# Block inverses in a gated DeltaNet layer: transposes that write row by row, and 32-column products on two row groups in turn

## The chip, the cores and the metric

The kernel runs on one core of a Trainium2 chip. The metric is the device time of one execution in microseconds; the median of several runs counts. One further execution was profiled, and every time inside the kernel below is from its trace.

## The reference, cut to what matters

The kernel computes a two-layer trunk for 256 tokens of width 2048: differential attention and a gated MLP with a short convolution, then a gated DeltaNet and a second such MLP. The change lies in the DeltaNet. For each of its 32 heads and each chunk of the sequence, the delta rule solves a unit lower triangular system:

```python
decay = jnp.exp(jnp.where(tril, g_c[..., :, None] - g_c[..., None, :], -jnp.inf))
low = jnp.where(strict, jnp.einsum('bhncd,bhnkd->bhnck', k_beta, k) * decay, 0.0)
a_mat = low + jnp.eye(CHUNK, dtype=low.dtype)
u = lax.linalg.triangular_solve(a_mat, v_beta, left_side=True, lower=True, unit_diagonal=True)
w = lax.linalg.triangular_solve(a_mat, k_beta * jnp.exp(g_c)[..., None], left_side=True, lower=True, unit_diagonal=True)
```

The kernel uses chunks of 128 tokens, which gives the same result, and forms the inverse of each 128 x 128 matrix instead of solving. There are 32 heads x 2 chunks = 64 such matrices.

## The kernel before, in words

**Large matmuls.** Nearly all of the work is dense: `dense` (lines 101 to 121) and `dense_tok` (127 to 142) multiply activations by weights that stream from memory in tiles of 512 KB. `weights` (line 76) issues the DMA into `raw`, ScalarE rounds it to `whi` (L88), VectorE subtracts to get `wlo` (L89), and TensorE takes three matmuls for each piece: high by high (L115), low by high (L116), high by low (L117); L137 to L139 are the same in `dense_tok`. `raw`, `whi` and `wlo` have three buffers each.

**Small work in between.** After each weight tile `dense` calls `tick` (line 71), which lets every generator in a background queue take one step. Attention, norms and the DeltaNet's own steps are such generators. So the small matmuls stand among the large ones in TensorE's program, and a `yield` is the place where large matmuls go between two dependent small steps. The program is then ordered by a scheduler with a model of the time, so that an engine's final order can differ a little from the order of the code.

**The inverses.** The DeltaNet goes through four blocks of four query heads, each query head with two value heads. Per block there are 8 value heads x 2 chunks = 16 matrices. `keys` puts the 32 x 32 diagonal pieces of all 16 matrices into one tile `Cc` of 128 partitions x 32 x 32: a partition's quarter (`quad[s]`, 32 partitions) tells which of a matrix's four diagonal pieces it holds. `invert` (line 511) transposes it on VectorE (L516), runs a substitution over 30 columns (L524, L527) and writes the result with two transposes:

- `ttc` (L531), indexed [partition, i, m]: the transposed inverses, with the matrix m last.
- `tcc` (L533), indexed [partition, c, m]: the inverses, read through a rearranged view, again with m last.

A VectorE transpose here turns every 32 x 32 piece (32 partitions by 32 elements) by itself. Since m is the last index, one matrix's row in `ttc` or `tcc` is 32 elements that lie 32 elements (128 bytes) apart.

**The levels.** `levels` (line 536) builds the full inverses from the diagonal pieces, for a group of two query heads (8 matrices) at a time, so twice per block and eight times in all:

1. GpSimd copies the diagonal pieces of the group into `TT` (L546, four quarters) and `Ta` (L548, two quarters).
2. `pp` (L552): for quarters s = 0 and s = 2, and the 8 matrices, a 32 x 32 product of a piece of `lt` with a piece of `tcc`. The result for quarter s goes to the PSUM partitions of quarter s + 1. It is copied to `pc`: quarter 1 by VectorE (L555), quarter 3 by ScalarE (L556).
3. `px` (L561): products of `pc` with `ttc`, read from quarters 1 and 3, into quarters 0 and 2. Then `py` (L565): products of `TT` with `pc`, quarter 1 alone. They go to `Ta` (L567, VectorE) and `TT` (L569, ScalarE).
4. `pq` (L573) and `pz` (L579): the 64 x 64 products of the next level, with copies L575 and L580.

In each product the first operand is loaded as weights (PEld in the profile) and the second one, the moving tile, is streamed. `tcc` in L552 and `ttc` in L561 are moving tiles; so is `pc` in L565. A *row group* is the quarter of TensorE's rows that matches the quarter of the partitions an operand is read from; a *column group* matches the quarter that the result goes to. The f32 products appear in the trace as two records each. All results of `small` are tiles `mp` of 512 f32 per partition, one PSUM bank, from a pool of four.

Of the kernel before, what the change touches and what calls it, by code (L numbers as in the profile page):

```python
# [26 lines left out]
class Trunk:  # L27
# [38 lines left out]
    def mp(self):  # L66
        return self.mps.tile([P, 512], F32, tag="mp", name="mp")
# [343 lines left out]
    def gdn(self, w_gate, w_in, w_z, w_out, nb, hb, gate_ap, const_ap, hot_ap, conv_col, ng, done):  # L411
# [7 lines left out]
        nc, tc, mp = self.nc, self.tc, self.mp  # L419
# [4 lines left out]
        with tc.tile_pool(name="gd", bufs=1) as gd:  # L424
# [16 lines left out]
            quad = [slice(32 * s, 32 * s + 32) for s in range(4)]  # L441
            flat = "p i c -> p (i c)"
            gates = {}

            def lin(ps):
                u = gd.tile([P, 2, T], F32, tag="u", name="u", bufs=2)
                self.merge(ps, u)
                return u

            def convs(u, tiles):  # L450
                c = gd.tile([P, 2, T], F32, tag="cv", name="cv", bufs=4)
                for i in range(2):
                    self.conv(c[:, i, :], u[:, i, :], [conv_col(t, tiles[i]) for t in range(4)], None)
                nc.scalar.activation(c, c, AF.Silu)  # L454
                return c
# [55 lines left out]
            def invert(cc, lqs, inv):  # L511

                while len(lqs) < 2 * hb:
                    yield
                x = gd.tile([P, 32, 32], F32, tag="s4", name="X", bufs=3)
                nc.vector.transpose(x.rearrange(flat), cc.rearrange(flat))  # L516
                t = gd.tile([P, 32, 32], F32, tag="s4", name="Ti", bufs=3)
                nc.vector.tensor_scalar(t, x, -1.0, None, ALU.mult)
                nc.vector.memset(t.rearrange(flat)[:, ::33], 1.0)
                for j in range(1, 31):  # L520
                    m = 31 - j
                    tmp = gd.tile([P, T], F32, tag="tmp", name="tmp", bufs=1)
                    w = tmp[:, :m * j].rearrange("p (i c) -> p i c", c=j)
                    nc.vector.tensor_tensor(  # L524
                        w, x[:, j + 1:, j:j + 1].to_broadcast([P, m, j]),
                        t[:, j:j + 1, :j].to_broadcast([P, m, j]), ALU.mult)
                    nc.vector.tensor_tensor(t[:, j + 1:, :j], t[:, j + 1:, :j], w, ALU.subtract)  # L527
                    if j % 3 == 0:
                        yield
                ttc = gd.tile([P, 32, 32], F32, tag="s4", name="ttc", bufs=3)  # L530
                nc.vector.transpose(ttc.rearrange(flat), t.rearrange(flat))  # L531
                tcc = gd.tile([P, 32, 32], F32, tag="s4", name="tcc", bufs=3)
                nc.vector.transpose(tcc, t.rearrange("p i c -> p c i"))  # L533
                inv += [ttc, tcc]

            def levels(TT, Ta, lts, ttc, tcc, m0):

                nm = 2 * len(lts)
                ms = slice(m0, m0 + nm)
                lview = [lt[:, :T].rearrange("p (t c) -> p t c", t=2) for lt in lts]  # L540

                def small(n):
                    return mp()[:, :nm * n].rearrange("p (m c) -> p m c", m=nm)

                for s in range(4):
                    nc.gpsimd.tensor_copy(TT[quad[s], :, quad[s]], ttc[quad[s], :, ms].rearrange("p i m -> p m i"))  # L546
                for s in range(2):
                    nc.gpsimd.tensor_copy(Ta[quad[s], :, quad[s]], tcc[quad[s], :, ms].rearrange("p c m -> p m c"))  # L548
                pp = small(32)
                for s in (0, 2):  # L550
                    for m in range(nm):
                        nc.tensor.matmul(pp[quad[s + 1], m, :], lview[m // 2][quad[s], m % 2, quad[s + 1]],  # L552
                                         tcc[quad[s], :, m0 + m], start=True, stop=True)
                pc = gd.tile([P, 2 * gv, 32], F32, tag="tmp", name="pc", bufs=1)
                nc.vector.tensor_copy(pc[quad[1]], pp[quad[1]])  # L555
                nc.scalar.copy(pc[quad[3]], pp[quad[3]])  # L556
                yield
                px = small(32)
                for s in (0, 2):
                    for m in range(nm):  # L560
                        nc.tensor.matmul(px[quad[s], m, :], pc[quad[s + 1], m, :], ttc[quad[s + 1], :, m0 + m],  # L561
                                         start=True, stop=True)
                py = small(32)
                for m in range(nm):
                    nc.tensor.matmul(py[quad[1], m, :], TT[quad[1], m, quad[1]], pc[quad[1], m, :],  # L565
                                     start=True, stop=True)
                nc.vector.tensor_scalar(Ta[quad[1], :, quad[0]], py[quad[1]], -1.0, None, ALU.mult)  # L567
                for s in (0, 2):
                    nc.scalar.mul(TT[quad[s], :, quad[s + 1]], px[quad[s]], -1.0)  # L569
                yield  # L570
                pq = small(64)
                for m in range(nm):
                    nc.tensor.matmul(pq[64:, m, :], lview[m // 2][:64, m % 2, 64:], Ta[:, m, :], start=True, stop=True)  # L573
                qs = gd.tile([P, 2 * gv, 64], F32, tag="lq", name="lq", bufs=1)
                nc.vector.tensor_copy(qs[64:], pq[64:])  # L575
                yield
                pz = small(64)
                for m in range(nm):
                    nc.tensor.matmul(pz[:64, m, :], qs[64:, m, :], TT[64:, m, 64:], start=True, stop=True)  # L579
                nc.vector.tensor_scalar(TT[:64, :, 64:], pz[:64], -1.0, None, ALU.mult)  # L580
# [11 lines left out]
            def group(gi, gr, lqs, inv, vt, ready, zts, acts):  # L592
# [5 lines left out]
                yield  # L598
                sub = lqs[2 * gr[0]:2 * gr[-1] + 2]
                yield from levels(TT, Ta, [lt for lt, _ in sub], *inv, 4 * gr[0])  # L600
                while len(ready) < len(gr):
                    yield
# [66 lines left out]
            for b in range(nb):  # L669
# [6 lines left out]
                for op, i in plan + [("v", i) for i in range(1, hb)]:  # L676
                    if op == "k":
                        hq = heads[i]
                        c = convs(lin(self.dense(w_in[hq * 2], KD, self.h_acts, HP)), (hq, nq + hq))
                        self.spawn(keys(hq, c, cc, 2 * i, lqs))  # L680
                        if i == hb - 1:
                            self.spawn(invert(cc, lqs, inv))
                    elif op == "z":
                        gr = groups[i]
                        zt = zts[i] = gd.tile([P, 2, gv, P], F32, tag="vz", name="zt", bufs=4)
                        ps = self.dense_tok(w_z[heads[gr[0]] // 2], KD, self.h_acts, 27 if b < 2 else 15)
                        for t in range(2):
                            nc.scalar.activation(zt[:, t].rearrange(flat), ps[:, t, :], AF.Silu,
                                                 scale=self.rstdc[:, t:t + 1])
                    else:  # L690
                        gi = i // gh
                        gr = groups[gi]
                        if i == gr[0]:
                            vt = gd.tile([P, 2, gv, P], F32, tag="vz", name="vt", bufs=4)
                            ready = []
                            self.spawn(group(gi, gr, lqs, inv, vt, ready, zts, acts))
                        hq = heads[i]
                        c = convs(lin(self.dense(w_in[hq * 2 + 1], KD, self.h_acts, HP)),
                                  (2 * nq + 2 * hq, 2 * nq + 2 * hq + 1))
                        self.spawn(to_tokens(c, vt, 2 * (i - gr[0]), ready))  # L700
# [204 lines left out]
```

## Time and profile before

| | us |
|---|---|
| median of 3 runs | 2669.3 |
| lowest and highest of them | 2666.23, 2669.54 |
| profiled execution, its own time | 2668.26 |
| its span, first to last instruction | 2666.5 |
| TensorE busy | 2650.4 |
| VectorE busy | 1847.8 |
| ScalarE busy | 1453.1 |
| GpSimd busy | 126.9 |

TensorE's granted clock was 0.999 in the mean. How to read the rows: in a timeline a row holds the start in us from the span's start, the length in us, engine, line, operation, tiles (written <- read), shapes and how many instructions in a row were merged; idle time before it, with what ended it, stands in brackets. In a row of groups the figures behind the bar are busy us, mean ns of one, and the idle us of the engine before them. In a table of stretches a row holds the stretch, its length, and for each engine the busy us with the number of instructions that were under way in it. PEld is the weight load. In the chain that ended last, each engine's share says how much of the span it held the end. The rows of an engine's order show a running number, line, operation, tiles and the form of the result.

### The profile page before, as it was taken

How to read it: one execution, taken by the hardware profiler on the slowest of the kernel's cores; microseconds unless marked ns; L12 is line 12 of the kernel's file. 1: busy time of each engine (PE TensorE's matmuls, PEld its weight loads, DVE VectorE, ACT ScalarE, POOL GpSimd, SP SyncE). 2: the span in 40 equal slices, each digit the busy share in tenths (PEclk: the TensorE clock that was granted, in tenths of full speed). 3: DMA queues.
4: the chain of work that ended last, by engine and by line, in shares of the span. 5: the costliest groups of instructions: out<-in, count | busy, mean ns of one | idle time of the engine just before them, and what ended most of it. 6: DMA issues, size and time to landing. Idle time of an engine off the chain costs nothing.

```text
span 2666.5 us, 53673 instructions
## 1 busy us (share of the span) xinstructions
PE 2650.4 (99%) x22352; PEld 2588.3 (97%) x22352; DVE 1847.8 (69%) x2719; ACT 1453.1 (54%) x1994; POOL 126.9 (5%) x221
## 2 busy tenths in 40 slices
PE   8999999999999999999999999999999999999999
PEld 8998899999999999999989989999999999999999
DVE  7776567777777555689787787688677777776444
ACT  6555555555555444584764674574565555554333
POOL 0000000000000000031011021021000000000000
PEclk9999999999999999999999999999999999999999
DMA  6555465665666666655354454455455655656665
GB/s 205 172 176 172 160 197 193 195 194 193 195 194 195 194 194 192 190 159 182 119 175 145 149 172 154 155 166 170 143 193 196 192 195 193 195 193 199 202 202 165
DMA packets 135461, 481.62 MB, mean 181 GB/s; under 512 B 15409, under 2 KB 18481, under 8 KB 135217
## 3 DMA queue, kind: packets, MB, share of 16 engines
q1 hardware_dynamic: 134064, 475.58, 55.6%
q8 instruction: 175, 2.87, 0.4%
q10 hardware_dynamic: 1152, 2.61, 0.3%
q14 instruction: 70, 0.57, 0.1%
HBM read 476.03 MB, written 2.10 MB: 179 GB/s over the span
## 4 chain that ended last, share of the span: by engine, by line
PE 94%; ACT 2%; DVE 2%; issue 1%; DMA 0%; POOL 0%; SPq 0%; DVEq 0%; ACTq 0%
PE ps L115 26%; PE ps L116 26%; PE ps L117 26%; PE ps L138 3%; PE ps L139 3%; PE ps L137 3%; PE mp L609 2%; DVE wlo L89 1%; ACT whi L88 1%; PE mp L225 1%; PE mp L552 1%; PE mp L561 0%; DVE cv L206 0%; ACT L454 0%; PE mp L573 0%
## 5 line engine op out<-in xcount | busy, mean ns | idle before, releaser
L89 DVE TENSOR_TENSOR wlo<-raw,whi 128x1024 fp32r<-128x1024 f32 (+2 forms) x909 | 1109.0, 1221 | 642.7 <-ACT whi L88 641.1
L88 ACT CAST whi<-raw 128x1024 fp32r<-128x1024 f32 (+2 forms) x909 | 948.4, 1044 | 1007.6 <-PE ps L117 837.8
L115 PE MATMUL ps<-h,whi 128*128 128x256 f32 x4304 | 1192.3, 277 | 8.4 <-ACT h L151 5.5
L116 PE MATMUL ps<-h,wlo 128*128 128x256 f32 x4304 | 1192.9, 277 | 3.1 <-DVE wlo L89 3.1
L117 PE MATMUL ps<-h,whi 128*128 128x256 f32 x4304 | 1191.7, 277 | 0.0
L115 PEld LDWEIGHTS ps<-h,whi 128*128 128x128 f32 x4304 | 808.8, 188 | 10.3 <-ACT h L151 5.5
L116 PEld LDWEIGHTS ps<-h,wlo 128*128 128x128 f32 x4304 | 809.4, 188 | 5.9 <-DVE wlo L89 4.0
L117 PEld LDWEIGHTS ps<-h,whi 128*128 128x128 f32 x4304 | 809.4, 188 | 0.5
L115 PE MATMUL ps<-ac,whi 128*128 128x256 f32 x1632 | 450.4, 276 | 0.0
L116 PE MATMUL ps<-ac,wlo 128*128 128x256 f32 x1632 | 450.3, 276 | 0.0
L117 PE MATMUL ps<-ac,whi 128*128 128x256 f32 x1632 | 450.2, 276 | 0.0
L115 PEld LDWEIGHTS ps<-ac,whi 128*128 128x128 f32 x1632 | 306.3, 188 | 0.0
L116 PEld LDWEIGHTS ps<-ac,wlo 128*128 128x128 f32 x1632 | 306.3, 188 | 0.0
L117 PEld LDWEIGHTS ps<-ac,whi 128*128 128x128 f32 x1632 | 306.2, 188 | 0.0
L138 PE MATMUL ps<-wlo,h 128*128 128x512 f32 x384 | 149.7, 390 | 0.2
L137 PE MATMUL ps<-whi,h 128*128 128x512 f32 x384 | 149.9, 391 | 0.0
L139 PE MATMUL ps<-whi,h 128*128 128x512 f32 x384 | 149.2, 389 | 0.0
L115 PE MATMUL ps<-oc,whi 128*128 128x256 f32 x512 | 143.9, 281 | 0.0
L117 PE MATMUL ps<-oc,whi 128*128 128x256 f32 x512 | 143.5, 280 | 0.0
L116 PE MATMUL ps<-oc,wlo 128*128 128x256 f32 x512 | 143.3, 280 | 0.0
L206 DVE SCALAR_TENSOR_TENSOR cv<-u,fcols,cv 128x255 f32<-128x255 f32 (+1 forms) x344 | 142.9, 478 | 0.0
L123 DVE TENSOR_TENSOR u<-ps,rstd 128x512 f32<-128x512 f32 x118 | 81.4, 690 | 38.2 <-PE ps L117 37.9
(202 smaller groups left out, 2232.1 us busy)
## 6 DMA issues: line engine op xcount, KB each, us to landing
raw<-w_up SPq DMA_DIRECT2D x344, 512.0 KB, 4.4
raw<-w_down SPq DMA_DIRECT2D x160, 512.0 KB, 4.1
raw<-w_in SPq DMA_DIRECT2D x128, 512.0 KB, 4.3
raw<-w_z SPq DMA_DIRECT2D x64, 512.0 KB, 3.7
raw<-w_out SPq DMA_DIRECT2D x64, 512.0 KB, 3.6
raw<-w_qk SPq DMA_DIRECT2D x63, 512.0 KB, 4.1
raw<-w_v SPq DMA_DIRECT2D x32, 512.0 KB, 3.7
raw<-w_o SPq DMA_DIRECT2D x32, 512.0 KB, 4.4
```

What stands on the lines that cost most here:

```text
L88: nc.scalar.copy(hi, raw)
L89: nc.vector.tensor_tensor(lo, raw, hi.bitcast(F32), ALU.subtract)
L115: nc.tensor.matmul(o, hi[:, k, s], a[:, 0, :], start=first, stop=False)
L116: nc.tensor.matmul(o, lo[:, k, s], a[:, 0, :], start=False, stop=False)
L117: nc.tensor.matmul(o, hi[:, k, s], a[:, 1, :], start=False, stop=last)
L123: self.nc.vector.tensor_tensor(u, ps[:, :, :T], self.rstd.unsqueeze(1).to_broadcast([P, 2, T]), ALU.mult)
L137: nc.tensor.matmul(ps[:, c, :], ah, hi[:, k, :], start=first, stop=False)
L138: nc.tensor.matmul(ps[:, c, :], ah, lo[:, k, :], start=False, stop=False)
L139: nc.tensor.matmul(ps[:, c, :], al, hi[:, k, :], start=False, stop=last)
L206: nc.vector.scalar_tensor_tensor(out[:, j:], u[:, :T - j], taps[n - 1 - j], out[:, j:], ALU.mult, ALU.add)
L225: last = self.nc.tensor.matmul(out, self.onesr, p[:, j], start=i + j == 0, stop=i + j == n)
L609: nc.tensor.matmul(p[:, v, :], l(v), r[:, v, :], start=i == 0, stop=i == len(terms) - 1)
```

## The change

Five edits, all in `invert` and `levels`:

- The transposes now write `ttc` as [partition, m, i] and `tcc` as [partition, m, c]: the output is given through a rearranged view, so that each matrix's row is 32 contiguous elements. The input of `ttc` stays contiguous, that of `tcc` stays rearranged.
- GpSimd's copies read these tiles without rearranging, and copy the quarters in the order 1, 3, 0, 2 into `TT`.
- `pp` runs over the matrices outside and the two quarters inside, so that consecutive products alternate between row groups 0 and 2.
- `px` likewise alternates between quarters 2 and 0 (row groups 3 and 1).
- `py` is computed in the same loop, one product after each two of `px`; both result tiles are taken ahead of it.

The number of instructions on each engine is the same. Lines behind the change have numbers two lower: `py` is L563, its copies L565 and L567, `pq` L571, `pz` L577.

```diff
                 ttc = gd.tile([P, 32, 32], F32, tag="s4", name="ttc", bufs=3)
-                nc.vector.transpose(ttc.rearrange(flat), t.rearrange(flat))
+                nc.vector.transpose(ttc.rearrange("p m i -> p i m"), t)
                 tcc = gd.tile([P, 32, 32], F32, tag="s4", name="tcc", bufs=3)
-                nc.vector.transpose(tcc, t.rearrange("p i c -> p c i"))
+                nc.vector.transpose(tcc.rearrange("p m c -> p c m"), t.rearrange("p i c -> p c i"))
...
-                for s in range(4):
-                    nc.gpsimd.tensor_copy(TT[quad[s], :, quad[s]], ttc[quad[s], :, ms].rearrange("p i m -> p m i"))
+                for s in (1, 3, 0, 2):
+                    nc.gpsimd.tensor_copy(TT[quad[s], :, quad[s]], ttc[quad[s], ms, :])
                 for s in range(2):
-                    nc.gpsimd.tensor_copy(Ta[quad[s], :, quad[s]], tcc[quad[s], :, ms].rearrange("p c m -> p m c"))
+                    nc.gpsimd.tensor_copy(Ta[quad[s], :, quad[s]], tcc[quad[s], ms, :])
                 pp = small(32)
-                for s in (0, 2):
-                    for m in range(nm):
+                for m in range(nm):
+                    for s in (0, 2):
                         nc.tensor.matmul(pp[quad[s + 1], m, :], lview[m // 2][quad[s], m % 2, quad[s + 1]],
-                                         tcc[quad[s], :, m0 + m], start=True, stop=True)
+                                         tcc[quad[s], m0 + m, :], start=True, stop=True)
...
-                px = small(32)
-                for s in (0, 2):
-                    for m in range(nm):
-                        nc.tensor.matmul(px[quad[s], m, :], pc[quad[s + 1], m, :], ttc[quad[s + 1], :, m0 + m],
+                px, py = small(32), small(32)
+                for m in range(nm):
+                    for s in (2, 0):
+                        nc.tensor.matmul(px[quad[s], m, :], pc[quad[s + 1], m, :], ttc[quad[s + 1], m0 + m, :],
                                          start=True, stop=True)
-                py = small(32)
-                for m in range(nm):
                     nc.tensor.matmul(py[quad[1], m, :], TT[quad[1], m, quad[1]], pc[quad[1], m, :],
                                      start=True, stop=True)
```

## The prediction

> **What bounds the kernel now.** I read the page first, then the chain that ended last, then the small products on TensorE's timeline. The page says that TensorE is the bound:
>
> ```profile
> span 2666.5 us, 53673 instructions
> ...
> PE 2650.4 (99%) x22352; PEld 2588.3 (97%) x22352; DVE 1847.8 (69%) x2719; ACT 1453.1 (54%) x1994; POOL 126.9 (5%) x221
> ...
> PE 94%; ACT 2%; DVE 2%; issue 1%; DMA 0%; POOL 0%; SPq 0%; DVEq 0%; ACTq 0%
> ```
>
> PE has work in 99% of the span and holds 94% of the chain, so a microsecond taken off TensorE is a microsecond off the end, as long as what feeds it keeps up. The groups of PE instructions show what the change touches:
>
> ```profile
> L561 PE MATMUL mp<-ttc,pc 32*32 32x32 f32 x256 | 14.0, 227 | 0.0
> L552 PE MATMUL mp<-tcc,lt 32*32 32x32 f32 x256 | 14.0, 227 | 0.0
> ...
> L565 PE MATMUL mp<-pc,TT 32*32 32x32 f32 x128 | 5.5, 192 | 0.0
> ```
>
> Each f32 product has two records, so 256 are 8 groups (four blocks, two groups each) of 16 products. All have idle 0.0: PE never waits for their operands. A mean of 227 ns is not a cost, as matmuls overlap; the cost is the distance between starts, which the timeline of one group gives. The first product, with the matmuls around it:
>
> ```profile
> 1246.36 0.28 PE L116 MATMUL ps<-h,wlo 128*128 128x256 f32 x1
> 1246.47 0.28 PE L117 MATMUL ps<-h,whi 128*128 128x256 f32 x1
> 1246.68 1.75 PE L552 MATMUL mp<-tcc,lt 32*32 32x32 f32 x32
> 1248.35 0.39 PE L115 MATMUL ps<-h,whi 128*128 128x256 f32 x1
> 1248.58 0.28 PE L116 MATMUL ps<-h,wlo 128*128 128x256 f32 x1
> ```
>
> From its first start to the next large matmul it takes 1248.35 - 1246.68 = 1.67 us. The second pair of products in the same group:
>
> ```profile
> 1252.32 1.58 PE L561 MATMUL mp<-ttc,pc 32*32 32x32 f32 x29
> 1253.68 0.21 PE L565 MATMUL mp<-pc,TT 32*32 32x32 f32 x1
> 1253.73 0.23 PE L561 MATMUL mp<-ttc,pc 32*32 32x32 f32 x1
> 1253.73 0.22 PE L565 MATMUL mp<-pc,TT 32*32 32x32 f32 x2
> 1253.79 0.23 PE L561 MATMUL mp<-ttc,pc 32*32 32x32 f32 x1
> 1253.80 0.22 PE L565 MATMUL mp<-pc,TT 32*32 32x32 f32 x2
> 1253.84 0.23 PE L561 MATMUL mp<-ttc,pc 32*32 32x32 f32 x1
> 1253.86 0.51 PE L565 MATMUL mp<-pc,TT 32*32 32x32 f32 x11
> 1254.30 0.38 PE L115 MATMUL ps<-h,whi 128*128 128x256 f32 x1
> ```
>
> It takes 1254.30 - 1252.32 = 1.98 us. The eight groups hold 8 x (1.67 + 1.98) = 29.2 us, and that is all the change can work on.
>
> Two things are to be seen in these rows. First, the last L561 starts are 1253.73, 1253.79, 1253.84, some 57 ns apart, while the last 11 L565 starts span 0.51 - 0.19 (the last one's own length) = 0.32 us in 10 steps, 32 ns apart. Both products are 32 x 32 x 32 in f32; what differs is the moving tile. L561 reads `ttc[quad, :, m]`, one element in 128 bytes; L565 reads `pc[quad, m, :]`, contiguous. Second, L565 (row group 1) starts while L561 (row group 3) is still running, and neither slows the other: L561 keeps 57 ns and L565 takes up 32 ns.
>
> **The change: the streams.** The moving tiles of L552 and L561 become contiguous, so I price their starts at 32 ns instead of 57. Then the order. On TensorE, first block, first group, the first product (`lt` numbers are heads; two products of each head per row group) before:
>
> ```order
> 9989 L117 MATMUL ps_14872<-h_75,whi_14921 128x256
> 9990 L552 MATMUL mp_14389<-tcc_14363,lt_13515 32x32 x2
> 9991 L552 MATMUL mp_14389<-tcc_14363,lt_13523 32x32 x2
> 9992 L552 MATMUL mp_14389<-tcc_14363,lt_13700 32x32 x2
> 9993 L552 MATMUL mp_14389<-tcc_14363,lt_13708 32x32 x2
> 9994 L552 MATMUL mp_14389<-tcc_14363,lt_13515 32x32 x2
> ```
>
> and now:
>
> ```order
> 9989 L117 MATMUL ps_14872<-h_75,whi_14921 128x256
> 9990 L552 MATMUL mp_14389<-tcc_14363,lt_13515 32x32 x4
> 9991 L552 MATMUL mp_14389<-tcc_14363,lt_13523 32x32 x4
> 9992 L552 MATMUL mp_14389<-tcc_14363,lt_13700 32x32 x4
> 9993 L552 MATMUL mp_14389<-tcc_14363,lt_13708 32x32 x4
> 9994 L115 MATMUL ps_14872<-h_75,whi_14921 128x256
> ```
>
> Each head's four products now stand together, and row groups 0 and 2 alternate inside them. Before, all of group 0 came first, and the two could overlap only where the one ended and the other began. That they do overlap there shows in the records of L552 in three stretches of 0.2 us, at its start, middle and end:
>
> ```profile
> 1246.90:1247.10 0.20, 0.20 (x7) 0.20 (x6) 1.00 0.00 0
> 1247.36:1247.56 0.20, 0.20 (x11) 0.20 (x9) 1.00 0.00 0
> 1247.80:1248.00 0.20, 0.20 (x7) 0.20 (x6) 1.00 0.00 0
> ```
>
> Seven in flight on one row group, eleven at the change-over, both writing the same tile `pp`, one PSUM bank, in different quarters of the partitions. The Trainium skill says against this change that different row tiles cannot use one PSUM bank at the same time ("TensorEngine Tiling (Array Packing)", Gotcha 1: PSUM Pressure); by that the two groups would be serial, and the sum would be that of the serial rival below. The eleven records speak against it.
>
> So for L552 I let two streams run side by side, 16 records each: 15 steps of 32 ns = 0.48, 0.02 for a slow first step (L565's first was 0.05), and 1254.30 - 1254.18 = 0.12 from the last start to the next large matmul (1254.18 is 1253.86 + 0.32). That is 0.62; with 0.02 for the second stream's late start 0.64 instead of 1.67: **1.03 us less per group, 8.2 over eight**.
>
> The second pair, same group, before:
>
> ```order
> 10030 L117 MATMUL ps_14872<-h_75,whi_14951 128x256
> 10031 L561 MATMUL mp_14427<-ttc_14361,pc_14406 32x32 x16
> 10032 L565 MATMUL mp_14444<-pc_14406,TT_13039 32x32 x8
> 10033 L115 MATMUL ps_14872<-h_75,whi_14993 128x256
> 10034 L116 MATMUL ps_14872<-h_75,wlo_14994 128x256
> ```
>
> and now (L563 is the old L565):
>
> ```order
> 10036 L561 MATMUL mp_14427<-ttc_14361,pc_14406 32x32 x2
> 10037 L563 MATMUL mp_14428<-pc_14406,TT_13039 32x32
> 10038 L561 MATMUL mp_14427<-ttc_14361,pc_14406 32x32 x2
> 10039 L563 MATMUL mp_14428<-pc_14406,TT_13039 32x32
> 10040 L561 MATMUL mp_14427<-ttc_14361,pc_14406 32x32 x2
> ```
>
> L563 has moved from behind all of L561 to every third place. Row group 3 has 16 records, but row group 1 has 32 (half of L561 and all of L563), which I take to be serial among themselves: 31 x 32 ns = 0.99 + 0.02 + 0.12 = 1.13, with 0.01 for the start 1.14 instead of 1.98: **0.84 less per group, 6.7 over eight**.
>
> **The transposes.** VectorE pays for the layout. `ttc` was written contiguous from a contiguous tile, `tcc` from a strided one:
>
> ```profile
> L533 DVE STREAM_TRANSPOSE tcc<-Ti 128x1024 f32<-128x1024 f32 x4 | 8.3, 2082 | 0.0
> ...
> L531 DVE STREAM_TRANSPOSE ttc<-Ti 128x1024 f32<-128x1024 f32 x4 | 5.0, 1244 | 0.1
> ```
>
> A strided write is not in these rows. Below, it could be free: 0 more. Nearest is the strided read, 2082 - 1244 = 0.84 us. Above, I let `tcc` pay reading and writing apart: 2 x 0.84 = 1.68 per block. Whether they add up is hinted at by the update of the substitution, strided on both sides in its first step and contiguous in its last:
>
> ```profile
> 1198.11 0.22 DVE L527 TENSOR_TENSOR Ti<-Ti,tmp 128x30 f32<-128x30 f32 x1
> ...
> 1240.20 0.19 DVE L527 TENSOR_TENSOR Ti<-Ti,tmp 128x30 f32<-128x30 f32 x1
> ```
>
> 0.03 us for 30 elements is 1 ns each, against 0.84 us / 1024 = 0.8 for a strided read alone: one penalty, not two. So I take 0.84 per block, all on `ttc`. It delays what is queued behind it on VectorE: `tcc`, which L552 waits for, and then the `wlo` subtractions (L89), which the large matmuls wait for.
>
> ```profile
> 1243.03 2.08 DVE L533 STREAM_TRANSPOSE tcc<-Ti 128x1024 f32<-128x1024 f32 x1
> 1245.04 0.64 DVE L123 TENSOR_TENSOR u<-ps,rstd 128x512 f32<-128x512 f32 x1
> ...
> 1623.17 2.08 DVE L533 STREAM_TRANSPOSE tcc<-Ti 128x1024 f32<-128x1024 f32 x1
> ...
> 1626.93 0.28 PE L552 MATMUL mp<-tcc,lt 32*32 32x32 f32 x2
> ```
>
> L552 follows `tcc` by 1246.68 - 1245.11 = 1.57 us in the first block and by 1626.93 - 1625.25 = 1.68 in the third. 0.84 fits; 1.68 would cost PE about 0.1 us a block. The second block had less room:
>
> ```profile
> 1423.97 2.08 DVE L533 STREAM_TRANSPOSE tcc<-Ti 128x1024 f32<-128x1024 f32 x1
> ...
> 1426.57 1.75 PE L552 MATMUL mp<-tcc,lt 32*32 32x32 f32 x32
> ```
>
> That is 0.52 us. But there the scheduler has moved VectorE's work. Before:
>
> ```order
> 1144 L123 TENSOR_TENSOR u<-ps,rstd 128x512
> 1145 L527 TENSOR_TENSOR Ti<-Ti,tmp 128x30
> 1146 L531 STREAM_TRANSPOSE ttc<-Ti 128x1024
> 1147 L533 STREAM_TRANSPOSE tcc<-Ti 128x1024
> 1148 L89 TENSOR_TENSOR wlo<-raw,whi 128x1024
> ```
>
> and now:
>
> ```order
> 1144 L527 TENSOR_TENSOR Ti<-Ti,tmp 128x30
> 1145 L531 STREAM_TRANSPOSE ttc<-Ti 128x32x32
> 1146 L533 STREAM_TRANSPOSE tcc<-Ti 128x32x32
> 1147 L89 TENSOR_TENSOR wlo<-raw,whi 128x1024
> 1148 L123 TENSOR_TENSOR u<-ps,rstd 128x512
> ```
>
> L123 (0.64 us) now stands behind the transposes, which gives back most of the 0.84; the rest, 0.20, fits into 0.52. Over four blocks I put the transposes at 0, at most 3 x 0.1 + (1.68 - 0.64 - 0.52) = 0.8 us. As to `wlo`, PE hardly ever waits for it (in the whole span 3.1 us in 4 waits):
>
> ```profile
>   PE ps L116: 3.1, 4
> ```
>
> **GpSimd and the copies.** GpSimd's copies start when `ttc` is there, so 0.84 later:
>
> ```profile
> 1243.17 7.58 POOL L546 COPY TT<-ttc 32x256 f32<-32x256 f32 x8 [48.34 <-DVE ttc L531]
> 1250.79 4.05 POOL L548 COPY Ta<-tcc 32x256 f32<-32x256 f32 x4
> ...
> 1258.24 0.27 PE L573 MATMUL mp<-Ta,lt 64*64 64x64 f32 x1
> ```
>
> The quarter that L563 needs is now copied first, long before 1253.68; the `Ta` copies end at 1254.84, and the 64-wide product that reads them (L573) starts at 1258.24. Reading contiguously they should be no slower. Cost 0, and 0 too for the copies to `pc`, whose shapes stay. No DMA is added or moved within its queue.
>
> **The sum.** 8.2 + 6.7 = 14.9 us. The profiled execution took 2668.3 (span 2666.5 and 1.8 around it): 2668.3 - 14.9 = 2653.4. The median of the three runs is 2669.3, 1.0 above it, so I say **2654**.
>
> **Rivals.**
> *Both tiles of row group 1 run side by side too.* L561 goes to column group 0 and L563 to column group 1. Then the second pair costs 0.64 as well: 1.34 less per group, 10.7 + 8.2 = 18.9, time 2649. No row shows two column groups of one row group together, either way.
>
> *Issue is the limit.* Between 1253.68 and 1253.86 the rows above hold 8 steps, 22 ns each, the densest I find. At that rate L552 is 31 x 22 ns + 0.14 = 0.82 and the pair 47 x 22 ns + 0.14 = 1.17: 0.85 + 0.81 = 1.66 less, 13.3 in all, 2655, which is the forecast again. The Trainium skill gives a floor of about 25 ns from start to start however small the matmul ("TensorE: Matmul & The Clock Gate", Wait — 56ns, not 53.3ns?); by it the saving would be 11.3 us, time 2657. The 22 ns, on two row groups, is below it.
>
> *No overlap beyond the change-over, or no gain from contiguous reads.* Serial at 32 ns, L552 is 31 x 32 ns + 0.14 = 1.13 and the pair 47 x 32 ns + 0.14 = 1.64: 0.54 + 0.34 less, 7.0 in all, 2661. If 57 ns is not the stride but the streams do run in pairs, L552 is 15 x 57 ns + 0.17 = 1.03 and the pair 16 x 57 + 16 x 32 ns + 0.14 = 1.56: 0.64 + 0.42, 8.5 in all, 2660. L565's 32 ns speaks against the second.
>
> *Each change of row group costs a drain: slower.* A change of shape does: from L117 at 1246.47 to L552 is 0.21 us, where L116 and L117 before it are 0.11 apart. If alternating cost such a 0.1, 15 changes in each product, 30 a group, are 3.0 us; on serial streams (0.88 less) that is 2.1 more, 17 over eight: 2685. It turns slower from 0.88 / 30 = 29 ns a change, and by more than 0.2% from (0.88 + 0.66) / 30 = 51 ns. Against it: L561 to L565 is such a change, and L565's first start (1253.68) falls between two of L561's.
>
> *The gain is taken back*: all later work in this layer is ordered anew, and waits of some 10 us would hide it. The chain's 2% each for ACT and DVE say that there is little to wait for.
>
> **How the numbers follow.** Forecast 0.50, an issue limit 0.12, both tiles side by side 0.11, serial or strided 0.13, drain 0.05, taken back 0.09. The range 2648 to 2662 holds the first four with their unknowns (0.8 for the transposes, some 1.5 for the scatter of the runs) and leaves out 0.14. About 0.2%, 5.3 us, is what a measurement of this kernel can tell from no change; all but the last two cases are faster by more, save a serial case at its edge: faster 0.84, same 0.11, slower 0.05.
>
> **What would show it.** In the changed profile: L552 from first start to next large matmul near 0.64 us, L561 with L563 near 1.14, their starts in one row group 32 ns apart; `ttc` near 2.08 us and `tcc` unchanged; no PE wait for `tcc`, `TT` or `Ta`. I am wrong if starts stay 57 ns apart, if a new row group starts only when the other is done, if a transpose takes over 3 us, or if PE gets idle time before L552 or L116.

## The result and the profile after

| kernel | median, us | runs, us | profiled execution, us (span) |
|---|---|---|---|
| before | 2668.53 | 2666.23 to 2669.54, 4 | 2668.26 (2666.5) |
| after | 2647.65 | 2646.20 to 2649.04, 4 | 2648.57 (2646.8) |

The median of before now has one run more than the 2669.3 it was forecast from. The ratio is 0.992, 95% interval 0.9909 to 0.9932. The time moved as forecast, but further: 2647.65 against 2654, and 0.35 us below the low end of the range. Between the profiled executions lie 19.7 us, between the medians 20.9.

The page of after, with the lines that answer to those of before:

```profile
span 2646.8 us, 53675 instructions
...
PE 2630.0 (99%) x22352; PEld 2568.2 (97%) x22352; DVE 1843.3 (70%) x2719; ACT 1452.6 (55%) x1994; POOL 112.9 (4%) x221
...
PE 94%; ACT 2%; DVE 2%; issue 1%; DMA 1%; POOL 0%; SPq 0%; DVEq 0%; ACTq 0%
```

TensorE (PE) is still the bound, with the same 94% of the chain. Its busy time fell by 20.4 us (2650.4 to 2630.0), the span by 19.7. The groups of PE, with busy time and mean ns of one ahead of the idle time:

```profile
L552 PE MATMUL mp<-tcc,lt 32*32 32x32 f32 x256 | 5.5, 192 | 0.0
L561 PE MATMUL mp<-ttc,pc 32*32 32x32 f32 x256 | 5.5, 192 | 0.0
L563 PE MATMUL mp<-pc,TT 32*32 32x32 f32 x128 | 5.5, 192 | 0.0
```

L552 and L561 were 14.0 each. The busy time of a line counts overlapping records once, so 5.5 for three lines of 256, 256 and 128 records says that all three spread over bursts of one length, 5.5 / 8 = 0.69 us with the last record's own end. The timeline of the first product, first group:

```profile
1248.39 0.28 PE L117 MATMUL ps<-h,whi 128*128 128x256 f32 x1
1248.60 0.69 PE L552 MATMUL mp<-tcc,lt 32*32 32x32 f32 x32
1249.22 0.38 PE L115 MATMUL ps<-h,whi 128*128 128x256 f32 x1
1249.44 0.28 PE L116 MATMUL ps<-h,wlo 128*128 128x256 f32 x1
```

From the first start to the next large matmul it is 1249.22 - 1248.60 = 0.62 us (0.623 to 0.625 in all eight groups) where it was 1.67. The second pair in the same group:

```profile
1254.19 0.22 PE L561 MATMUL mp<-ttc,pc 32*32 32x32 f32 x2
1254.20 0.21 PE L563 MATMUL mp<-pc,TT 32*32 32x32 f32 x1
1254.24 0.20 PE L561 MATMUL mp<-ttc,pc 32*32 32x32 f32 x2
1254.26 0.19 PE L563 MATMUL mp<-pc,TT 32*32 32x32 f32 x1
1254.28 0.20 PE L561 MATMUL mp<-ttc,pc 32*32 32x32 f32 x2
...
1254.69 0.20 PE L561 MATMUL mp<-ttc,pc 32*32 32x32 f32 x2
1254.70 0.19 PE L563 MATMUL mp<-pc,TT 32*32 32x32 f32 x1
1254.82 0.38 PE L115 MATMUL ps<-h,whi 128*128 128x256 f32 x1
```

Three records start within about 0.015 us and the next three some 0.03 later (0.032 by the trace's start times), to the end: 1254.82 - 1254.19 = 0.63 us (0.630 in all eight groups) where it was 1.98. L563 and the L561 record of the same row group start in the same round: they are not serial. Over eight groups the products gave 8 x (1.67 - 0.62) = 8.4 and 8 x (1.975 - 0.630) = 10.8, together 19.2 of the 19.7 us.

VectorE's transposes in the groups of after:

```profile
L533 DVE STREAM_TRANSPOSE tcc<-Ti 128x1024 f32<-128x1024 f32 x4 | 8.7, 2173 | 0.0
...
L531 DVE STREAM_TRANSPOSE ttc<-Ti 128x1024 f32<-128x1024 f32 x4 | 8.4, 2106 | 0.1
```

A strided write costs `ttc` 2106 - 1244 = 862 ns; `tcc`, strided on both sides now, costs 2173 - 2082 = 91 ns more than with the strided read alone. The rows around them in the second block, VectorE's ahead of PE's:

```profile
1417.32 2.17 DVE L533 STREAM_TRANSPOSE tcc<-Ti 128x1024 f32<-128x1024 f32 x1
```

```profile
1420.25 0.69 PE L552 MATMUL mp<-tcc,lt 32*32 32x32 f32 x32
```

L552 starts 1420.25 - 1419.49 = 0.76 us after `tcc` is there. In the four blocks it is 0.66, 0.76, 0.81 and 0.83 us, so nothing waits for it; the longest waits of PE in after say the same, with microseconds in total, times and the longest:

```profile
PE ps L115 <- ACT h L151: 5.7, 1, 5.7
PE ps L115 <- ACT whi L88: 3.3, 2, 2.6
PE ps L116 <- DVE wlo L89: 3.1, 4, 1.4
```

No `tcc`, `TT` or `Ta` is among them, and `wlo` has its 3.1 us in 4 waits as before. GpSimd's copies in after:

```profile
1245.98 5.27 POOL L546 COPY TT<-ttc 32x256 f32<-32x256 f32 x8 [49.50 <-DVE ttc L531]
1251.29 2.01 POOL L548 COPY Ta<-tcc 32x256 f32<-32x256 f32 x4
```

They start 2.8 us later than in before and end at 1253.30 where it was 1254.84. The lines' own views have minimum, median and maximum in ns:

```profile
L546 POOL COPY TT<-ttc x32: 391/399/1524, 1246.0 to 1825.0; 32x256 f32<-32x256 f32 x32
```

```profile
L548 POOL COPY Ta<-tcc x16: 391/492/1299, 1251.3 to 1827.1; 32x256 f32<-32x256 f32 x16
```

Reading contiguously, the median copy takes 399 and 492 ns where both took 758.

### The profile page after: what moved, and what is told of

Read it like the earlier page. It is cut to its first block, busy times and chain, and to the rows that moved or that the text cites. A ratio compares the mean times of both kernels' runs of the same rounds, so it can differ in the third digit from the quotient of the medians.

```text
span 2646.8 us, 53675 instructions
## 1 busy us (share of the span) xinstructions
PE 2630.0 (99%) x22352; PEld 2568.2 (97%) x22352; DVE 1843.3 (70%) x2719; ACT 1452.6 (55%) x1994; POOL 112.9 (4%) x221
## 4 chain that ended last, share of the span: by engine, by line
PE 94%; ACT 2%; DVE 2%; issue 1%; DMA 1%; POOL 0%; SPq 0%; DVEq 0%; ACTq 0%
PE ps L115 27%; PE ps L117 27%; PE ps L116 27%; PE ps L138 3%; PE ps L139 3%; PE ps L137 3%; PE mp L607 2%; DVE wlo L89 1%; ACT whi L88 1%; PE mp L225 1%; DVE cv L206 0%; DMA raw<-w_in 0%; PE mp L577 0%; PE mp L571 0%; ACT L454 0%
## 5 line engine op out<-in xcount | busy, mean ns | idle before, releaser
L89 DVE TENSOR_TENSOR wlo<-raw,whi 128x1024 fp32r<-128x1024 f32 (+2 forms) x909 | 1105.6, 1217 | 640.9 <-ACT whi L88 638.6
L116 PE MATMUL ps<-h,wlo 128*128 128x256 f32 x4304 | 1192.3, 277 | 3.1 <-DVE wlo L89 3.1
L116 PEld LDWEIGHTS ps<-h,wlo 128*128 128x128 f32 x4304 | 809.8, 188 | 5.6 <-DVE wlo L89 4.0
L116 PE MATMUL ps<-ac,wlo 128*128 128x256 f32 x1632 | 450.3, 276 | 0.0
L116 PEld LDWEIGHTS ps<-ac,wlo 128*128 128x128 f32 x1632 | 306.2, 188 | 0.0
L116 PE MATMUL ps<-oc,wlo 128*128 128x256 f32 x512 | 142.8, 279 | 0.0
```

Source lines behind the costliest of these rows:

```text
L89: nc.vector.tensor_tensor(lo, raw, hi.bitcast(F32), ALU.subtract)
L116: nc.tensor.matmul(o, lo[:, k, s], a[:, 0, :], start=False, stop=False)
```

## The experiments

Theory before the runs: each pair of a row group and a column group is a stream of its own, 32 ns from start to start with contiguous moving tiles and 57 with one element in 128 bytes; streams run side by side. Rival of the prediction's own step: all records of one row group are one stream.

**Layout without order.** The changed transposes and copies, with the loops of before:

```diff
-                for m in range(nm):
-                    for s in (0, 2):
+                for s in (0, 2):
+                    for m in range(nm):
...
-                px, py = small(32), small(32)
-                for m in range(nm):
-                    for s in (2, 0):
+                px = small(32)
+                for s in (0, 2):
+                    for m in range(nm):
...
+                py = small(32)
+                for m in range(nm):
```

> The new layout of ttc and tcc with the old order of the products. Theory (each pair of row group and column group is a stream of its own, products start in program order): contiguous moving tiles give 32 ns a step, but streams overlap only where one ends and the next begins, some 3 steps. L552 about 31 x 32 ns - 0.10 + 0.14 = 1.03 us, L561 with L565 about 47 x 32 ns - 0.20 + 0.14 = 1.44 us; 1.18 us less per group than before, so about 2659. Rival (57 ns was not the stride): L552 stays at 1.67 and the pair at 1.98, about 2668.

It took 2657.90 us (2656.03 to 2659.16, 5 runs) beside 2668.12 for before; ratio 0.9957, interval 0.9943 to 0.9972. Its timeline, the first product and then the pair:

```profile
1246.17 1.09 PE L552 MATMUL mp<-tcc,lt 32*32 32x32 f32 x32
1247.19 0.38 PE L115 MATMUL ps<-h,whi 128*128 128x256 f32 x1
...
1251.14 1.00 PE L561 MATMUL mp<-ttc,pc 32*32 32x32 f32 x29
...
1252.07 0.57 PE L565 MATMUL mp<-pc,TT 32*32 32x32 f32 x13
1252.57 0.38 PE L115 MATMUL ps<-h,whi 128*128 128x256 f32 x1
```

1.02 and 1.43 us, where the theory had 1.03 and 1.44. Contiguous tiles do set the step, so 57 ns was the stride.

**Order without layout.** The changed loops, with the transposes and copies of before:

```diff
-                nc.vector.transpose(ttc.rearrange("p m i -> p i m"), t)
+                nc.vector.transpose(ttc.rearrange(flat), t.rearrange(flat))
...
-                                         tcc[quad[s], m0 + m, :], start=True, stop=True)
+                                         tcc[quad[s], :, m0 + m], start=True, stop=True)
...
-                        nc.tensor.matmul(px[quad[s], m, :], pc[quad[s + 1], m, :], ttc[quad[s + 1], m0 + m, :],
+                        nc.tensor.matmul(px[quad[s], m, :], pc[quad[s + 1], m, :], ttc[quad[s + 1], :, m0 + m],
```

> The old layout with the new order. Theory of streams by row and column group: L552 15 x 57 ns + 0.17 = 1.03 us, L561 with L563 the same, 1.05 us, though row group 1 has two column groups; 1.55 us less per group, about 2656. Rival (products of one row group are serial): the pair 16 x 57 + 16 x 32 ns + 0.14 = 1.56 us, about 2660. Rival (alternating does not work on strided tiles): L552 stays at 1.67 us.

It took 2653.78 us (2651.94 to 2657.55, 4 runs), ratio 0.9946, interval 0.9931 to 0.9961. From its timeline:

```profile
1248.19 1.07 PE L552 MATMUL mp<-tcc,lt 32*32 32x32 f32 x32
1249.20 0.38 PE L115 MATMUL ps<-h,whi 128*128 128x256 f32 x1
...
1254.17 0.23 PE L561 MATMUL mp<-ttc,pc 32*32 32x32 f32 x2
...
1255.20 0.39 PE L115 MATMUL ps<-h,whi 128*128 128x256 f32 x1
```

1.01 and 1.03 us, where the theory had 1.03 and 1.05 (over the eight groups the pair takes 1.015 to 1.026, in the mean 1.02). If row group 1 were one stream, its 16 records at 57 ns and 16 at 32 would need the 1.56 that the prediction worked out for this case. The four kernels side by side, per group and over eight:

| | L552 | pair | eight groups | gain there | gain in the medians |
|---|---|---|---|---|---|
| before | 1.67 | 1.975 | 29.2 | | |
| layout alone | 1.02 | 1.430 | 19.6 | 9.6 | 10.2 |
| order alone | 1.01 | 1.02 | 16.2 | 13.0 | 14.3 |
| both | 0.62 | 0.630 | 10.0 | 19.2 | 20.8 |

The two do not add up (9.6 + 13.0 = 22.6), since the one shortens the steps and the other their number, in the same bursts. (The last row's median gain is that of a later run of the changed kernel, below.)

**The step in dispute: L563 behind L561.** One line more than the changed kernel:

```diff
+                for m in range(nm):
                     nc.tensor.matmul(py[quad[1], m, :], TT[quad[1], m, quad[1]], pc[quad[1], m, :],
```

> As the changed kernel, but L563 (here L564) again follows all of L561. Theory of streams: L561 takes 16 steps on two streams, L564 16 more on one, less some 3 steps of overlap: 31 x 32 ns - 0.10 + 0.15 = 1.04 us instead of 0.63, about 3.3 us more in all. The theory of serial row groups, which the prediction took, gives 1.14 us here and had given 1.14 for the changed kernel.

2651.42 us in one run, span 2649.6, 2.8 above that of the changed kernel. The pair in its timeline:

```profile
1253.86 0.60 PE L561 MATMUL mp<-ttc,pc 32*32 32x32 f32 x26
...
1254.39 0.57 PE L564 MATMUL mp<-pc,TT 32*32 32x32 f32 x13
1254.89 0.38 PE L115 MATMUL ps<-h,whi 128*128 128x256 f32 x1
```

1.03 us, as the theory of streams had it (1.04): L561 first, then L564 (the old L563), with a short overlap between them. Folding L563 into the loop of L561 is worth 1.03 - 0.63 = 0.40 us a group, 3.2 over eight.

**One row group, two column groups.** Both L552 products read row group 0 (so the lower half of the inverses is built from the wrong piece):

```diff
-                        nc.tensor.matmul(pp[quad[s + 1], m, :], lview[m // 2][quad[s], m % 2, quad[s + 1]],
-                                         tcc[quad[s], m0 + m, :], start=True, stop=True)
+                        nc.tensor.matmul(pp[quad[s + 1], m, :], lview[m // 2][quad[0], m % 2, quad[s + 1]],
+                                         tcc[quad[0], m0 + m, :], start=True, stop=True)
```

> In L552 both products of a matrix read row group 0; they still go to column groups 1 and 3 (the lower half of the inverses is then built from the wrong piece). Theory that each pair of row and column group is a stream, and the rival that the column group alone is: L552 stays at 0.62 us. Rival that a row group has one stream: 31 x 32 ns + 0.15 = 1.14 us, 4 us more in all.

```profile
1247.32 0.69 PE L552 MATMUL mp<-tcc,lt 32*32 32x32 f32 x32
1247.95 0.38 PE L115 MATMUL ps<-h,whi 128*128 128x256 f32 x1
```

The timeline shows 0.63 by these rounded rows, 0.623 by the trace's start times, as with two row groups; the run took 2647.24 us. A row group is not a stream by itself.

**Two row groups, one column group.** Both products go to column group 1, in two banks. The second isn't used, and the last quarter of `pc` is copied from `tcc` instead:

```diff
-                pp = small(32)
+                pp, p2 = small(32), small(32)
...
-                        nc.tensor.matmul(pp[quad[s + 1], m, :], lview[m // 2][quad[s], m % 2, quad[s + 1]],
+                        nc.tensor.matmul((p2 if s else pp)[quad[1], m, :], lview[m // 2][quad[s], m % 2, quad[s + 1]],
...
-                nc.scalar.copy(pc[quad[3]], pp[quad[3]])
+                nc.scalar.copy(pc[quad[3]], tcc[quad[3], ms, :])
```

> In L552 the two products of a matrix come from row groups 0 and 2 but both go to column group 1, into two PSUM banks; the second is not used, and pc's last quarter is copied from tcc instead (the output changes). Theory that each pair of row and column group is a stream: L552 stays at 0.62 us. Rival that the column group is what must differ: 31 x 32 ns + 0.15 = 1.14 us.

The second group of the first block in its timeline (in the first group two L561 records stand among those of L552, as they need not wait for `pc` there):

```profile
1261.57 0.69 PE L552 MATMUL mp<-tcc,lt 32*32 32x32 f32 x32
1262.20 0.55 PE L586 MATMUL mp<-con,cv 128*128 128x128 f32 x3
```

0.63 us again (0.625 by start times), time 2648.27. A column group is not a stream by itself either.

**Four streams.** A second pair of products, from row group 1 to column group 0 and from 3 to 2, in a bank that nobody reads; 64 records in a burst where there were 32:

```diff
+                    for s in (1, 3):
+                        nc.tensor.matmul(p2[quad[s - 1], m, :], lview[m // 2][quad[s], m % 2, quad[s - 1]],
+                                         tcc[quad[s], m0 + m, :], start=True, stop=True)
```

> L552 gets a second pair of products per matrix (L555), from row groups 1 and 3 to column groups 0 and 2, into a bank of its own that nobody reads: 64 records instead of 32. Theory: four streams side by side, started some 7 ns apart, 28 ns a round, still under 32: about 0.65 us, and 0.2 us in all. Rival (issue at 10.6 ns a record, the densest of the changed kernel, is the limit): 63 x 10.6 ns + 0.14 = 0.81 us, 1.5 us in all.

2648.90 us, span 2647.1: twice the products in L552's place for 0.3 us more span than the changed kernel's. Its timeline:

```profile
1247.80 0.22 PE L552 MATMUL mp<-tcc,lt 32*32 32x32 f32 x2
1247.81 0.22 PE L555 MATMUL mp<-tcc,lt 32*32 32x32 f32 x2
1247.85 0.20 PE L552 MATMUL mp<-tcc,lt 32*32 32x32 f32 x2
1247.86 0.20 PE L555 MATMUL mp<-tcc,lt 32*32 32x32 f32 x2
...
1248.34 0.21 PE L555 MATMUL mp<-tcc,lt 32*32 32x32 f32 x2
1248.48 0.38 PE L115 MATMUL ps<-h,whi 128*128 128x256 f32 x1
```

0.68 us: near the theory's 0.65, far from the 0.81 of its rival. Sixteen rounds of four starts take some (0.68 - 0.12) / 16 = 0.035 us a round in the mean, 9 ns a start; by the start times the first rounds are 32 ns apart, as with two streams, and the later ones longer. At the prediction's 22 ns a start, 64 would have needed 63 x 0.022 + 0.12 = 1.5 us.

**What the cover is worth.** To see how much VectorE time the products' wait for `tcc` would bear, `ttc` is transposed twice in one kernel and `tcc` in another; the first one's edit:

```diff
-                nc.vector.transpose(ttc.rearrange("p m i -> p i m"), t)
+                for _ in range(2):
+                    nc.vector.transpose(ttc.rearrange("p m i -> p i m"), t)
```

> The first transpose is done twice, 2.11 us more on VectorE per block. Theory: the cover of the transposes is what lies between the end of tcc and L552, 0.66 to 0.83 us in the changed kernel, so PE waits about 2.11 - 0.75 = 1.35 us before the first L552 of each block, 5.4 us in all, about 2654. Rival (transposes are hidden in whatever length): no wait, 2648.6.

> The column transpose is made twice in a row, so 4 x 2.17 = 8.7 us more on VectorE ahead of what reads tcc, which has only 0.66 to 0.83 us to spare in the changed kernel. Theory (the VectorE work is beside TensorE's, and the recorded order puts the products behind it): the products stand some 15 to 90 rows later in TensorE's order and no wait for tcc arises, so 2647 to 2651 us. Rival 1 (the time to spare is what hides the transposes): TensorE waits 2.17 - 0.75 = 1.4 us in each of four blocks or more, 2654 or above. Rival 2 (VectorE bounds this stretch): 8.7 us more, 2657.

2650.37 us (granted clock 1.000) and 2657.34 (0.999), one run each. The changed kernel's eight runs, four of them further below, took 2645.85 to 2646.73 us at 1.000 and 2648.57 to 2649.29 at 0.999, so the one costs some 4.1 us and the other 8.4. The scheduler did not leave the rest in place: it put the second `ttc` transpose behind `tcc`, and the second `tcc` one behind two to four other instructions, with the products later in TensorE's order. So the first kernel didn't delay `tcc` at all and missed what it was made for; neither its theory (about 2654) nor the rival (2648.6) was met. The waits of PE, of the first and of the second kernel:

```profile
PE ps L116 <- DVE wlo L89: 5.8, 8, 1.4
```

```profile
PE ps L116 <- DVE wlo L89: 6.4, 12, 1.4
...
PE mp L553 <- DVE tcc L534: 0.2, 1, 0.2
```

The group of `tcc` in the second kernel is VectorE's part, 17.7 us where the changed kernel has 8.7:

```profile
L534 DVE STREAM_TRANSPOSE tcc<-Ti 128x1024 f32<-128x1024 f32 x8 | 17.7, 2214 | 0.0
```

The theory was right in that nearly no wait for `tcc` arises (0.2 us), and wrong in the time: 2647 to 2651 was expected of the second kernel, and it came out where rival 2 put it: nearly all of VectorE's 9.0 us more came into the time. The named waits hold 6.4 + 0.2 - 3.1 = 3.5 us of that (2.7 of the 4.1 in the first kernel), nearly all for `wlo`.

Starts show more of it than idle time. A large matmul's record lasts 0.28 us where the next usually starts after 0.11, so a late start counts as idle only from 0.17 us on. In the DeltaNet of the changed kernel L116, which reads `wlo`, starts once over 0.32 us after the record ahead of it and 0.05 us after a subtraction of L89 has ended; beyond the usual distance that is 0.6 us. The first kernel has five such starts with 3.8 us, the second nine with 5.1. So waiting for `wlo` holds some 3.3 of the 4.1 us and 4.5 of the 8.4. Another 0.8 of the 8.4 had come by 1199 us, ahead of the first of these transposes; some 3 us stay open. What follows: VectorE's time here is not free without bound, even where the products don't wait.

**Both groups in one burst.** Each burst pays for its ends: 0.21 from the last large matmul to its first start, 0.12 behind its last start, and 0.22 to the second large matmul where 0.11 is usual. Here a block's two groups send each stage together, 64 records for 32, called once per block (the copies to `pc` get one tile for both groups, and each of the two 64-wide products waits one turn of the scheduler more):

```diff
-            def levels(TT, Ta, lts, ttc, tcc, m0):
+            def levels(parts, ttc, tcc):
...
+                pps = [small(32) for _ in gs]
+                for pp, (TT, Ta, lview, m0) in zip(pps, gs):
+                    for m in range(nm):
+                        for s in (0, 2):
...
-                yield from levels(TT, Ta, [lt for lt, _ in sub], *inv, 4 * gr[0])
+                if gi == 0:
+                    yield from levels([(TTs[i], Tas[i], lqs[4 * i:4 * i + 4], 8 * i) for i in range(2)], *inv)
+                    inv.append(None)
+                while len(inv) < 3:
+                    yield
```

> Both groups of a block go through the levels together, so that equal products stand together: 32-wide ones in one burst instead of two in all four blocks, the last 64-wide ones in three. Theory: what remains of a burst is mostly its ends, 0.72 + 0.11 us beyond the normal step for 0.51 us of steps, so each burst saved gives about 0.33 us: 11 x 0.33 = 3.6 us less than the changed kernel, about 2644 to 2645. Rival (PSUM buffers or late copies make PE wait): no gain or a loss.

2644.67 us (2642.74 to 2645.62, 5 runs), as the theory had it, ratio 0.991, interval 0.9897 to 0.9924. To set it against the changed kernel itself, both ran once more on one chip:

> The changed kernel once more, on the same chip as the kernel with both groups of a block in one burst: 2647 to 2649 us expected, span about 2646.8. It is here only so that the next run has a neighbour.

> Both groups of a block send each stage in one burst. The bursts' ends should be paid once and not twice: in the run before, one burst of 64 records took 1.130 us + 0.206 ahead, where two bursts take 2 x (0.623 + 0.206) = 1.658, so 0.32 less per block at L555, about as much at L569 and L571 (2 x (0.630 + 0.206) + one second matmul's 0.11), and in three of four blocks as much at L593: 4 x 0.65 to 4 x 0.95 = 2.6 to 3.8 us less than the changed kernel. Rival: the difference between the two earlier runs (2.98 us) lay between chips, and the same chip shows less than 1 us.

The changed kernel took 2647.64 us (2645.85 to 2649.29, 4 runs; ratio 0.9921, interval 0.9906 to 0.9935), the fused one 2643.79 (2642.76 to 2644.95, 4 runs; ratio 0.9908, interval 0.9891 to 0.9924). The intervals overlap, as both ratios carry the scatter of before; but all four runs of the one lie below all four of the other, by 3.85 us between the medians. This version beats both kernels. From its timeline, in the run on the same chip:

```profile
1246.11 1.20 PE L555 MATMUL mp<-tcc,lt 32*32 32x32 f32 x64
1247.24 0.38 PE L115 MATMUL ps<-h,whi 128*128 128x256 f32 x1
```

1.13 us for 64 records, against twice 0.62. By the traces' starts the fused stages take 0.5 us less over the four blocks in L552's place, 1.0 in that of L561 and L563, and 1.0 in that of L577, which went together in three blocks of four: 2.5, just under the 2.6 to 3.8 expected. In the first block the fused pair takes 1.45 us where the other three take 1.14: the second group's products start 0.24 us after the last of the first group's, and the trace names ScalarE's copy to `pc` as what they wait for. What the spared second matmuls and the rest brought isn't taken apart.

## Why the prediction was wrong in size

*The streams of L552*: right. 0.64 was forecast and 0.62 measured, for the reason given: 15 steps of 32 ns, two row groups side by side, writing one bank. The Trainium skill's rule that different row tiles cannot use one PSUM bank at the same time ("TensorEngine Tiling (Array Packing)", Gotcha 1: PSUM Pressure) does not hold here: L552's 32 records in 0.62 us are on two row groups, all in `pp`, and with a bank for each row group they took 0.625.

*The second pair*: the step that failed is "row group 1 has 32 (half of L561 and all of L563), which I take to be serial among themselves", 1.14 us and 6.7 over eight. It measured 0.630 and 10.8, 4.1 us more. The rival "Both tiles of row group 1 run side by side too" is what happened: counted from the profiled execution, as the rivals are, it gives 2668.3 - 18.9 = 2649.4, and the profiled execution took 2648.57. The run with one row group shows it by itself (32 records on one row group in 0.623 us), and the one with L563 behind L561 shows its price from the other side. I had given it 0.11, though I wrote that no row spoke for either case; without a row the two deserved like chances, and a range that reached clearly below 2649. The Trainium skill did have a rule for it: row and column tiles compose, so that small products on different (row, column) tiles run together ("TensorE: Matmul & The Clock Gate", Why this matters for your kernels). The 0.623 us for 32 records on one row group and two column groups agree, and the 0.683 for 64 records on four tiles.

*Transposes*: right. 0.84 more for `ttc` was forecast and 0.86 came; nearly none for `tcc`, and 0.09 came; no wait of PE. It stayed inside the spare time before L552, now 0.66 to 0.83 us. The two kernels with a doubled transpose, 4.1 and 8.4 us slower, show that much more would not have been free.

*GpSimd at 0*: right in effect. The copies even became faster (399 and 492 ns for 758), and no wait of PE ends on them.

*The sum*: 8.4 + 10.8 = 19.2 against 14.9. Where the other 0.5 of the 19.7 us lies isn't taken apart. Between the medians it is 20.9 instead of the 19.7 between the profiled executions: two of the four runs after, at a mean granted clock of 1.000, took 2646.20 and 2646.73, the other two, at 0.999, 2648.57 and 2649.04. The traces show what lies between: those at 0.999 have at least one stretch of 3.4 us at half the granted clock (0.51 from 1445.6 to 1449.0 us in before, 0.50 from 21.1 to 24.5 in after), in which large matmuls start 0.213 us apart instead of 0.113; those at 1.000 have none before their last 2 us. Both profiled executions have one, so the 19.7 compare like with like. From 2653.4 + 1.0 = 2654.4 to 2647.65 it is 6.8 us: 4.3 from the products, 0.5 elsewhere, 1.2 between profiled executions and medians, and 0.8 because the median of before came out below the 2669.3 that the forecast started from. That the last three all went the same way is chance; without the 4.1 us of the second pair the median would have stayed inside the range.

*The other rivals*: an issue limit of 22 ns fell with the starts 7 to 9 ns apart, a drain at each change of row group with bursts that have no gap at 15 such changes, no overlap or no gain from contiguous reads with the two half changes, each of which gained by itself. Nothing was taken back by waits.

## What to carry to other kernels

Small products that go to different places of the array (row group and column group) were streams of their own here: order them so that the streams alternate in short rounds, and count the records of the longest stream, not those of a row group. Keep moving tiles contiguous in the order in which a product reads them, and let an engine that has time to spare pay for the layout, after measuring how much it has. Where a step has no row for or against it, split the chances evenly and let the range hold both.

## What the runs showed of the hardware

- Starts within one stream of 32 x 32 x 32 f32 products are 32 ns apart with a contiguous moving tile and 57 ns with one element in 128 bytes. Starts of different streams are 7 ns apart in the trace, and four streams take 35 ns a round in the mean. The Trainium skill's floor of about 25 ns from start to start ("TensorE: Matmul & The Clock Gate", Wait — 56ns, not 53.3ns?) holds here within a stream, not between streams.
- Two products on one row group and two column groups, two on one column group and two row groups, and two on different groups of both kinds took the same 0.62 us.
- A VectorE transpose of 128 x 1024 f32 took 1.24 us contiguous, 2.11 with the strided write, 2.08 with the strided read and 2.17 with both.
- A burst of small products between large ones delays these by 0.21 + 0.62 + 0.22 - 2 x 0.11 = 0.83 us, of which its 15 steps are 0.48; the rest is paid at its ends, which were the same 0.21, 0.12 and 0.22 us in bursts of 32, 48, 64 and 96 records with contiguous moving tiles.
